# A decoder block on one core: the second convolution pair on the unnormalised input, GpSimd's powers in written order, and two pairs with one seven-product chunk

## The chip, the cores and the metric

The kernel runs on one core of one Trainium2 chip. The metric is device time in microseconds (us), from one launch of the whole program. Before the change the median of three runs is 2031.65 us (2030.2 to 2033.77). The engines are named as in the profile: PE is TensorE (PEld its weight loads), DVE is VectorE, ACT is ScalarE, POOL is GpSimd, SP the queue that issues most of the loads.

## The reference, cut to what matters

One layer of a decoder trunk on 256 tokens of width 2048 (float32):

```
h = rmsnorm(x, norm_mix)                       # x * rsqrt(mean(x^2) + eps) * gain
proj = h @ w_in                                # 2048 columns in, 15360 out
   -> differential attention (8 heads, two maps each, causal, rmsnorm per head)
   -> u = ca * sigmoid(cb); causal depthwise convolution of 31 taps over u; layernorm; silu
   -> retention in chunks of 128 (8 heads), normalised per head, times silu(rg)
   -> three sigmoid gates
x = x + (g0*(ya @ w_br0) + g1*(yb @ w_br1) + g2*(yr @ w_br2)) @ w_out
x = x + cross_attention(rmsnorm(x), rmsnorm(mem))      # 4 heads, 256 memory tokens, wq wkv wo
x = x + (silu(a) * b) @ w2,   a, b = rmsnorm(x) @ w13  # hidden 5632
out = rmsnorm(x, norm_final)
```

The row factor of an rmsnorm can be taken out of a product: (x * r * gain) @ W equals r times ((x * gain) @ W), so a product may be computed on x * gain and multiplied by r when it leaves the accumulator.

## The kernel before

**Products.** Every float32 operand is split into a high part (rounded to fp32r) and a low part (the rest), and a product is three matmuls: high by high, high by low, low by high. A weight matrix is cut into column blocks of 512, and each block into four chunks of 512 rows; a chunk is loaded in halves of 512 KB (tile `raw`, ten buffers, issued by SP through `ld`). ACT makes the high part (`wh`, a cast), DVE the low part (`wl`, a subtraction); both have five buffers. A unit is one such half or one factor of a chunk, with its matmuls; a half with both token tiles is 12 matmuls of 128x512, a factor of a seven-product chunk is 6. `emit_unit` (line 306) first builds the parts of the four units that follow and then writes the matmuls of its own.

**Pairs of column blocks.** `pair` (line 405) computes two column blocks at once. Each of its four chunks is of one of two kinds, by the letters of a mode string. An N chunk is eight half-products: four units of 12 matmuls. An S chunk (`quad_jobs`, line 332) is seven factors, p1 to p7, of 6 matmuls each, put together by sums; it needs two DVE sums on `raw` (in f2 and f3), and two more loads of 512 KB that add into a `raw` tile on their way, issued by POOL through `gd`: f2 issues one for p7, f6 one for p4. An S chunk also needs sums of the activations (`factors`). The factors p1, p5, p6 and p7 are gathered in one-bank accumulators (`tp`), the two blocks in two two-bank accumulators (`mm`, two buffers). The names are `MODES2 = "SSNN"`, `MODES1 = "SNNN"`, `MODES0 = "NNNN"`. `pair_n` (line 481) is for a pair on activations that are not normalised yet: no S chunk; its block 0 is complete after 12 of its 16 units, and is evacuated there, and `after(c)` tells when a chunk of activations has been read for the last time.

**Normalising between pairs.** `normalise` (line 640) takes chunks of x * gain, multiplies them by the row factor r, and makes new high and low parts; it starts at its chunk `at`. `spread` brings r into the layout of the chunks by a small matmul. `Rstd` waits for r; `rstd_of` (line 515) computes r on DVE (scale and eps) and then POOL (a power of -0.5).

**The stages.** The kernel starts with blocks 8 and 6 of w_in (`pair_n`, the gate and the value of the first half of the convolution's channels) on `xa`, then blocks 9 and 7 (the second half) on the normalised `xn`, as two plain blocks; then the blocks of retention and attention (plain), the gates and branches (pairs), the memory's keys and values (four `pair`s on `mm`, line 1182), w_out, cross attention, and the feed-forward part: 11 pairs of w_13 (line 1419 and before; the first is a `pair_n` on `x2T`) with w_2 between.

**Tasks.** Work beside the products (evacuations, transposes, the convolution, statistics) is written as generators. `pump` (line 142) moves each of them one `yield` after every unit; `drain` runs one to its end. So a `yield` more puts what follows one unit later in the program.

**What sets the order.** The program is planned before it runs: for each engine the planner orders the instructions by a model of time, and among ready ones takes the one written first. Two rules hold against that freedom. `keep_in_program_order` ties an instruction to the one written before it on its engine: `gd` and `ld` always use it, the power in `rstd_of` does not. And the buffers of one pool tag are handed out in the order in which the program first writes them: of the 392 tiles of tag s4 (28 buffers, the tile `s` of the profile) none is first written ahead of one that is written earlier in the program.

```
L519  nc.gpsimd.tensor_tensor(out=dst, in0=v, in1=nhalf[:, :w], op=ALU.pow)
L881  pair_n([w_in[8, c] ...], [w_in[6, c] ...], xa, ev_cb(0, rsx), ev_ca(0, rsx),
             normalise(xa, xn, Rstd(rsx, lambda: drain(st_task)), (), 1))
L883  win(9, 7, MODES0, ev_cb(1), ev_ca(1))
```

Of the kernel before, what the change touches and what calls it, by code (L numbers as in the profile page):

```python
# [13 lines left out]
ALU = mybir.AluOpType  # L14
AX = mybir.AxisListType

D = 2048
# [40 lines left out]
def trunk(ctx, tc, xT, xtok, memT, memtok, w_in, w_br, w_out, w_q, w_kv, w_o, w_13, w_2,  # L58
# [88 lines left out]
    def drain(g):  # L147
        if g in first:
            drain(first.pop(g))
        if g in active:  # L150
            settle(cap[0] - wants[g], g)
            while step(g):
                pass
# [327 lines left out]
    def pair_n(W0, W1, acts, evac0, evac1, after):  # L481

        ps0, ps1 = {}, {}
        u0, u1 = [], []
        for c in range(2):
            u0 += half_jobs(ps0, [W0[c]], [acts[c]])
            u1 += half_jobs(ps1, [W1[c]], [acts[c]])
            call(lambda c=c: after(c))
        u0 += half_jobs(ps0, W0[2:], acts[2:])
        call(lambda: evac0(ps0["m"]))  # L490
        for c in range(2, 4):
            u1 += half_jobs(ps1, [W1[c]], [acts[c]])
            call(lambda c=c: after(c))
        call(lambda: evac1(ps1["m"]))
        close(u0 + u1)
# [19 lines left out]
    def rstd_of(dst, src, scale, w):  # L515

        v = TN(w)
        ve.tensor_scalar(out=v, in0=src, scalar1=scale, scalar2=EPS, op0=ALU.mult, op1=ALU.add)
        nc.gpsimd.tensor_tensor(out=dst, in0=v, in1=nhalf[:, :w], op=ALU.pow)  # L519

    def actT_part(a, r, g, c, ks):
        if a.hi is None:
# [173 lines left out]
    def tok_stats(src, dst, eng):  # L696

        parts = cpool.tile([P, 4, 2], F32, name=nm("parts"))
        for n in range(4):
            r = S4([P, 2, 512])  # L700
            eng(out=r, in_=src[n])
            yield
            sumsq(r, parts[:, n, :])
            yield
        ss = TN(2)
        ve.tensor_reduce(out=ss, in_=parts.rearrange("p n t -> p t n"), op=ALU.add, axis=AX.X)
        rstd_of(dst, ss, 1.0 / D, 2)

    def start_task():
        for c in range(2, 4):  # L710
# [71 lines left out]
    def ev_cb(i, rs=None):  # L782
        def f(ps):
            if rs is not None:
                drain(st_task)
            cv["s", i] = act(ps, AF.Sigmoid, rs)
        return f
# [50 lines left out]
    def conv_norm():  # L838
        ys = [cv[("y", 0)], cv[("y", 1)]]
        bn = TN(24)  # L840
        for t in range(2):
            for i in range(2):
                o = (2 * t + i) * 6
                ve.bn_stats(out=bn[:, o:o + 6], in_=ys[i][:, t, :])
        mv = TN(4)
        for t in range(2):
            ve.bn_aggr(out=mv[:, 2 * t:2 * t + 2], in_=bn[:, 12 * t:12 * t + 12])
        rs = TN(2)
        rstd_of(rs, mv.rearrange("p (t s) -> p t s", t=2)[:, :, 1], 1.0, 2)
        yield  # L850
        for i in range(2):
            for t in range(2):
                ve.tensor_scalar(out=ys[i][:, t, :], in0=ys[i][:, t, :], scalar1=mv[:, 2 * t:2 * t + 1],
                                 scalar2=rs[:, t:t + 1], op0=ALU.subtract, op1=ALU.mult)
        yield
        for i in range(2):
            z = cv["z", i] = S4([P, 4, 256])
            src = blk(ys[i])
            for pr in range(2):
                tp = TP().rearrange("p (k c) -> p k c", k=2)  # L860
                for k in range(2):
                    for t in range(2):
                        pe.transpose(tp[:, k, t * P:(t + 1) * P], src(2 * pr + k, t), ident)
                yield 1
                for k in range(2):
                    c = 4 * i + 2 * pr + k
                    sc.activation(z[:, 2 * pr + k, :], tp[:, k, :], AF.Silu, scale=pc("lg", c), bias=pc("lb", c))
                tp = None
                yield
# [3 lines left out]
    def win(n0, n1, modes, evac0, evac1):  # L873
# [3 lines left out]
        else:  # L877
            block(w_in, n0, xn, evac0)
            block(w_in, n1, xn, evac1)

    pair_n([w_in[8, c] for c in range(4)], [w_in[6, c] for c in range(4)], xa, ev_cb(0, rsx), ev_ca(0, rsx),  # L881
           normalise(xa, xn, Rstd(rsx, lambda: drain(st_task)), (), 1))
    win(9, 7, MODES0, ev_cb(1), ev_ca(1))  # L883


    def ev_rope(store, key, half, ro):
# [47 lines left out]
    def ret_task(g, st):  # L934
        drain(st["qt"])
        drain(st["kt"])
        q, k, v, sg, dm = st["q"], st["k"], st["v"], st["g"], st["d"]
        o = S4([P, 2, 512])
        yield
        for h in range(4):  # L940
            s = TP()
            pe.matmul(s[:, 0:256], k[:, h, 0:P], q[:, h, :], start=True, stop=True)
            pe.matmul(s[:, 256:384], k[:, h, P:256], q[:, h, P:256], start=True, stop=True)
            yield 1
            p = SM(384)
            ve.tensor_tensor(out=p[:, 0:256], in0=s[:, 0:256], in1=dm[:, h, :], op=ALU.mult)
            ve.tensor_tensor(out=p[:, 256:384], in0=s[:, 256:384], in1=dm[:, h, 0:P], op=ALU.mult)
            s = None
            yield
            c = slice(h * P, (h + 1) * P)  # L950
            av = TP()
            pe.matmul(av[:, 0:P], p[:, 0:P], v[:, 0, c], start=True, stop=True)
            pe.matmul(av[:, P:256], p[:, P:256], v[:, 0, c], start=True, stop=False)
            pe.matmul(av[:, P:256], p[:, 256:384], v[:, 1, c], start=False, stop=True)
            yield 1
            sc.copy(o[:, :, c], av[:, 0:256].rearrange("p (t c) -> p t c", t=2))
            av = None
        q = k = v = dm = None
        st.clear()
        yield  # L960
        mv = TN(16)
        for t in range(2):
            for h in range(4):
                bn = TN(6)
                ve.bn_stats(out=bn, in_=o[:, t, h * P:(h + 1) * P])
                i = (4 * t + h) * 2
                ve.bn_aggr(out=mv[:, i:i + 2], in_=bn)
            yield
        rs = TN(8)
        rstd_of(rs, mv.rearrange("p (t s) -> p t s", s=2)[:, :, 1], 1.0, 8)  # L970
        yield
        for t in range(2):
            for h in range(4):
                i = 4 * t + h
                c = slice(h * P, (h + 1) * P)
                ve.tensor_scalar(out=o[:, t, c], in0=o[:, t, c], scalar1=mv[:, 2 * i:2 * i + 1],
                                 scalar2=rs[:, i:i + 1], op0=ALU.subtract, op1=ALU.mult)
            ve.tensor_tensor(out=o[:, t, :], in0=o[:, t, :], in1=sg[:, t, :], op=ALU.mult)
            yield
        sg = None  # L980
        yield from transposed(yr[g], blk(o), lambda kt: pc("gn", 4 * g + kt))
# [16 lines left out]
    def diff_task(g, st):  # L998
# [64 lines left out]
        ms = TN(8)  # L1063
        ve.tensor_reduce(out=ms, in_=sq.rearrange("p t (h c) -> p (t h) c", h=4), op=ALU.add, axis=AX.X)
        rs = TN(8)
        rstd_of(rs, ms, 1.0 / P, 8)
        yield
        for t in range(2):
            for h in range(4):
# [107 lines left out]
    for m, dst in ((0, kM), (4, vM)):  # L1177
        for h in (0, 2):
            if m == 4 and h == 2:
                call(mT_factors)  # L1180
            w0, w1 = ([w_kv[m + n, c] for c in range(4)] for n in (h, h + 1))
            pair(w0, w1, mm, MODES2, ev_kv(dst[h]), ev_kv(dst[h + 1]))
    call(lambda: [setattr(a, k, None) for a in mm for k in ("hi", "lo", "shi", "slo")])


    def residual(W, acts, xin, aT, gname, rs, parts, spill=None):

        xs = [None] * 4

        def ev(nb):  # L1190
            def f(ps):
                r = xin(nb)
                ve.tensor_tensor(out=r, in0=ps, in1=r, op=ALU.add)
                xs[nb] = r
                if spill is not None:
                    xs[nb] = None
                    gd(out=spill[nb], in_=r)

                def gen():
                    sumsq(r, parts[:, nb, :])  # L1200
                    yield from transposed(aT[nb], blk(r), lambda kt: pc(gname, 4 * nb + kt))
                aT[nb].task = spawn(gen())
                if nb == 3:
                    def gen2():
                        yield
                        yield
                        ss = TN(2)
                        ve.tensor_reduce(out=ss, in_=parts.rearrange("p n t -> p t n"), op=ALU.add, axis=AX.X)
                        rstd_of(rs, ss, 1.0 / D, 2)
                    rst[gname] = spawn(gen2())  # L1210
            return f
        return xs, ev
# [197 lines left out]
    def ffn_pairs(r):  # L1410
        for i in r:
            w0, w1 = ([w_13[n, c] for c in range(4)] for n in (i, 11 + i))
            if i == 0:
                pair_n(w0, w1, x2T, ev_a(i, rs2), ev_b(i, rs2), after2)
            else:
                pair(w0, w1, x2n, MODES2, ev_a(i), ev_b(i))

    def load_x2(nbs):
        for nb in nbs:
# [157 lines left out]
```

## Time and profile before

| | |
|---|---|
| three timed runs | 2031.65 us median (2030.2 to 2033.77) |
| the profiled execution's own time | 2031.24 us |
| its span, first to last instruction | 2029.5 us |
| mean granted TensorE clock | 0.991 |
| instructions with a record | PE 9069, DVE 2049, ACT 1344, POOL 176 |
| PE, DVE, ACT, POOL busy | 1990.1, 1680.8, 1122.2, 133.1 us |

All times inside the program are from the start of the span. A granted clock of 1.00 is the higher of TensorE's two levels (2.4 GHz), 0.50 the lower one (1.2 GHz). A line such as L86 is that of a helper through which most instructions pass, so rows are told apart by their tiles. The profile of one execution has records of nearly all instructions; a few matmuls can be missing.

### The profile page before, as it was taken

The page shows a single profiled execution, that of the slowest core. Times are in us where ns is not written, and L with a number is a line of the kernel's source. Part 1 is how long each engine was busy: PE and PEld are TensorE (multiplying, and loading weights), DVE is VectorE, ACT ScalarE, POOL GpSimd, SP SyncE. Part 2 cuts the span into 40 slices and gives each one's busy share as a digit, 9 for nine tenths or more (in the row PEclk, how much of TensorE's full clock was granted, in tenths as well). Part 3 has the DMA queues.
Part 4 walks back from the last instruction along what each step waited for, and adds up shares of the span by engine and source line. Part 5 has one row for each costly group of instructions (what it writes and reads, how often), then busy time and mean ns, then how long its engine had stood idle before and what let it go on. Part 6 is the DMA issues. An engine that isn't in the chain of part 4 may idle for free.

```text
span 2029.5 us, 25287 instructions
## 1 busy us (share of the span) xinstructions
PE 1990.1 (98%) x9069; PEld 1641.5 (81%) x9069; DVE 1680.8 (83%) x2049; ACT 1122.2 (55%) x1344; POOL 133.1 (7%) x176
## 2 busy tenths in 40 slices
PE   9999999999999999999999999998999999999998
PEld 7788888888788887778888888886888888878886
DVE  6996689777887787988988565898988899889974
ACT  6434343547465556555656554665655566555653
POOL 0000000000100001011010000100011101011000
PEclk9999999999999999999999999998999999999999
DMA  9555555554677788689999643967899888998891
GB/s 370 189 194 188 176 181 165 181 168 149 176 220 239 243 257 248 226 240 280 284 279 307 208 159 125 288 184 212 226 283 297 257 260 237 289 295 258 262 318 67
DMA packets 128861, 465.97 MB, mean 230 GB/s; under 512 B 14432, under 2 KB 14688, under 8 KB 128736
## 3 DMA queue, kind: packets, MB, share of 16 engines
q1 hardware_dynamic: 105552, 380.46, 53.2%
q0 software_dynamic: 23040, 83.90, 19.5%
q8 instruction: 71, 1.16, 0.2%
q14 instruction: 54, 0.44, 0.1%
q10 hardware_dynamic: 144, 0.01, 0.0%
HBM read 451.73 MB, written 12.58 MB: 229 GB/s over the span
## 4 chain that ended last, share of the span: by engine, by line
PE 50%; issue 9%; DVE 6%; DMA 5%; POOL 1%; ACT 1%; ACTq 0%; POOLq 0%; DVEq 0%
PE mm L86 38%; PE tp L86 12%; DMA raw<-in_w 4%; DVE wl L86 3%; DVE s L86 3%; DMA raw<-in_w_out 1%; DVE raw L86 1%; ACT wh L86 1%; POOL raw L94 1%; DMA s<-in_memtok 0%; DMA raw<-in_w_in 0%; ACT s L86 0%; ACTq L1572 0%; POOL s L94 0%; POOL x2d L94 0%
## 5 line engine op out<-in xcount | busy, mean ns | idle before, releaser
L86 PE MATMUL mm<-wh,s 128*128 128x512 f32 x4528 | 1440.1, 393 | 22.5 <-ACT wh L86 8.7
L86 ACT CAST wh<-raw 128x1024 fp32r<-128x1024 f32 (+1 forms) x861 | 893.6, 1051 | 754.3 <-PE mm L86 462.7
L86 DVE TENSOR_TENSOR wl<-raw,wh 128x1024 fp32r<-128x1024 f32 (+1 forms) x861 | 1030.1, 1220 | 265.2 <-ACT wh L86 252.0
L86 PEld LDWEIGHTS mm<-wh,s 128*128 128x128 f32 x4528 | 854.5, 189 | 204.8 <-ACT wh L86 13.5
L86 PE MATMUL mm<-wl,s 128*128 128x512 f32 x2264 | 889.5, 393 | 7.6 <-DVE wl L86 7.4
L86 PEld LDWEIGHTS mm<-wl,s 128*128 128x128 f32 x2264 | 428.0, 189 | 100.7 <-DVE wl L86 13.2
L86 PE MATMUL tp<-wh,s 128*128 128x512 f32 x896 | 298.5, 392 | 0.0
L86 PEld LDWEIGHTS tp<-wh,s 128*128 128x128 f32 x896 | 168.2, 188 | 34.7 <-issue 0.3
L86 PE MATMUL tp<-wl,s 128*128 128x512 f32 x448 | 174.5, 389 | 0.0
L86 DVE TENSOR_TENSOR s<-s,s 128x1024 f32<-128x1024 f32 (+4 forms) x144 | 141.4, 990 | 5.8 <-ACT s L86 4.0
L86 DVE TENSOR_TENSOR raw<-raw,raw 128x1024 f32<-128x1024 f32 x104 | 126.0, 1220 | 0.5
L86 DVE TENSOR_TENSOR s<-tp,s 128x512 f32<-128x512 f32 (+1 forms) x166 | 110.0, 685 | 19.0 <-PE tp L86 14.2
L86 DVE SCALAR_TENSOR_TENSOR s<-s,prm_t,s 128x256 fp32r<-128x256 f32 (+24 forms) x256 | 105.5, 469 | 0.0
L86 DVE TENSOR_TENSOR s<-mm,s 128x1024 f32<-128x1024 f32 (+1 forms) x71 | 84.4, 1190 | 21.7 <-PE mm L86 21.3
L86 PEld LDWEIGHTS tp<-wl,s 128*128 128x128 f32 x448 | 84.2, 188 | 16.8
L86 ACT ACTIVATE s<-s 128x512 f32<-128x512 f32 (+1 forms) x60 | 46.2, 771 | 64.3 <-DVE s L86 53.9
L94 POOL DMA_DIRECT2D raw<-in_w x56 | 49.4, 882 | 439.4 <-DVE wl L86 187.9
L86 PE MATMUL tp<-cst_t,s 128*128 128x128 f32 x408 | 57.2, 273 | 0.0
L86 PEld LDWEIGHTS tp<-cst_t,s 128*128 128x128 f32 x408 | 48.7, 141 | 9.2 <-issue 0.5
L86 PE MATMUL tp<-s,s 128*128 128x256 f32 (+4 forms) x348 | 54.1, 314 | 0.0
L86 PEld LDWEIGHTS tp<-s,s 128*128 128x128 f32 (+1 forms) x348 | 46.4, 189 | 5.9 <-issue 0.7
L86 ACT COPY s<-tp 128x512 f32<-128x512 f32 (+1 forms) x69 | 35.8, 529 | 21.5 <-PE tp L86 20.0
(88 smaller groups left out, 499.3 us busy)
## 6 DMA issues: line engine op xcount, KB each, us to landing
raw<-in_w SPq DMA_DIRECT2D x264, 512.0 KB, 6.7
raw<-in_w_in SPq DMA_DIRECT2D x239, 512.0 KB, 4.5
raw<-in_w_kv SPq DMA_DIRECT2D x64, 512.0 KB, 6.3
raw<-in_w POOLq DMA_DIRECT2D x56, 512.0 KB, 8.5
raw<-in_w_br SPq DMA_DIRECT2D x48, 512.0 KB, 5.9
raw<-in_w_out SPq DMA_DIRECT2D x32, 512.0 KB, 7.8
raw<-in_w_q SPq DMA_DIRECT2D x32, 512.0 KB, 4.9
raw<-in_w_o SPq DMA_DIRECT2D x32, 512.0 KB, 4.0
```

The source lines that it names most:

```text
L86: i = f(*a, **k)
L94: tc.keep_in_program_order(nc.gpsimd.dma_start(**kw))
```

## The change

In five edits:

```diff
 def rstd_of(dst, src, scale, w):
         v = TN(w)
         ve.tensor_scalar(out=v, in0=src, scalar1=scale, scalar2=EPS, op0=ALU.mult, op1=ALU.add)
-        nc.gpsimd.tensor_tensor(out=dst, in0=v, in1=nhalf[:, :w], op=ALU.pow)
+        yield
+        yield
+        tc.keep_in_program_order(nc.gpsimd.tensor_tensor(out=dst, in0=v, in1=nhalf[:, :w], op=ALU.pow))
...
-        rstd_of(dst, ss, 1.0 / D, 2)
+        yield from rstd_of(dst, ss, 1.0 / D, 2)
...
-    pair_n([w_in[8, c] for c in range(4)], [w_in[6, c] for c in range(4)], xa, ev_cb(0, rsx), ev_ca(0, rsx),
-           normalise(xa, xn, Rstd(rsx, lambda: drain(st_task)), (), 1))
-    win(9, 7, MODES0, ev_cb(1), ev_ca(1))
+    for n, after in ((0, lambda c: None),
+                     (1, normalise(xa, xn, Rstd(rsx, lambda: drain(st_task)), ()))):
+        pair_n([w_in[8 + n, c] for c in range(4)], [w_in[6 + n, c] for c in range(4)], xa,
+               ev_cb(n, rsx), ev_ca(n, rsx), after)
...
-            pair(w0, w1, mm, MODES2, ev_kv(dst[h]), ev_kv(dst[h + 1]))
+            pair(w0, w1, mm, MODES2 if m or h else MODES1, ev_kv(dst[h]), ev_kv(dst[h + 1]))
...
-                pair(w0, w1, x2n, MODES2, ev_a(i), ev_b(i))
+                pair(w0, w1, x2n, MODES1 if i == 1 else MODES2, ev_a(i), ev_b(i))
```

The other callers of `rstd_of` (the convolution's layernorm, retention, differential attention, the two residuals) are changed to `yield from` in the same way. The second pair is evacuated with the row factor, as the first: two ACT instructions instead of one, and two DVE instructions instead of one; the normalisation starts in the second pair, after its first chunk.

## Rows read from the trace of the kernel before

**Rows 1.** Page, part 1: busy time, share of the span, instructions.
```profile
PE 1990.1 (98%) x9069; PEld 1641.5 (81%) x9069; DVE 1680.8 (83%) x2049; ACT 1122.2 (55%) x1344; POOL 133.1 (7%) x176
```

**Rows 2.** Waits of PE, whole span: us in total, times, longest.
```profile
PE mm L86 <- ACT wh L86: 8.7, 9, 3.6
PE mm L86 <- DVE wl L86: 7.4, 12, 1.5
PE mm L86 <- DVE s L86: 7.0, 1, 7.0
PE mm L86 <- ACT s L86: 6.7, 2, 4.7
```

**Rows 3.** Stretches of 40 us: busy (instructions) by engine, granted clock, DMA.
```profile
40.00:80.00 40.00, 35.34 (x151) 28.74 (x150) 34.36 (x42) 21.04 (x23) 0.70 (x1) 0.91 0.64 233
...
520.00:560.00 40.00, 35.27 (x152) 28.23 (x152) 30.31 (x46) 21.00 (x31) 3.37 (x3) 0.93 0.66 193
560.00:600.00 40.00, 40.00 (x175) 33.04 (x175) 33.80 (x32) 24.14 (x26) 1.69 (x2) 0.98 0.73 220
...
680.00:720.00 40.00, 40.00 (x178) 33.14 (x177) 31.59 (x29) 21.40 (x22) 1.70 (x2) 1.00 0.73 224
...
840.00:880.00 40.00, 34.32 (x139) 26.49 (x138) 36.64 (x41) 19.91 (x22) 3.43 (x4) 0.87 0.67 166
...
1400.00:1440.00 40.00, 32.98 (x137) 26.77 (x136) 34.93 (x39) 19.75 (x22) 3.42 (x4) 0.87 0.69 188
```

**Rows 4.** Instructions in order of time, all engines, 40 to 90 us.
```profile
53.84 1.04 ACT L86 CAST s<-s 128x1024 fp32r<-128x1024 f32 x1
...
56.19 1.26 ACT L86 ACTIVATE s<-mm,rsx 128x512 f32<-128x512 f32 x2
...
57.51 0.79 PE L86 MATMUL mm<-wh,s 128*128 128x512 f32 x1 [4.66 <-ACT s L86]
```

**Rows 5.** POOL's instructions in order of time: start, us, idle before.
```profile
33.41 0.70 POOL L519 TENSOR_TENSOR rsx<-tn,nhalf 128x2 f32<-128x2 f32 x1 [32.56 <-DVE tn L86]
...
528.88 0.86 POOL L94 DMA_DIRECT2D raw<-in_w_in  x1 [14.54 <-DVE wl L86]
545.35 1.66 POOL L519 TENSOR_TENSOR tn<-tn,nhalf 128x8 f32<-128x8 f32 x1 [15.61 <-DVE tn L86]
546.97 0.89 POOL L94 DMA_DIRECT2D raw<-in_w_in  x1
...
804.80 1.62 POOL L519 TENSOR_TENSOR rsm<-tn,nhalf 128x2 f32<-128x2 f32 x1 [8.02 <-DVE tn L86]
...
1319.27 0.71 POOL L519 TENSOR_TENSOR rs<-tn,nhalf 128x2 f32<-128x2 f32 x1 [1.43 <-DVE tn L86]
```

**Rows 6.** Chain of waits, 500 to 570 us: start, us, what.
```profile
546.97 7.08 DMA raw<-in_w_in
```

**Rows 7.** ACT in order of time, around 1353 us.
```profile
1353.60 1.27 ACT L86 ACTIVATE s<-mm,rs 128x512 f32<-128x512 f32 x2
```

**Rows 8.** Waits of PE, 840 to 880 us.
```profile
PE mm L86 <- DVE wl L86: 3.1, 3, 1.5
PE mm L86 <- ACT s L86: 2.1, 1, 2.1
PE mm L86 <- ACT wh L86: 0.5, 1, 0.5
```

**Rows 9.** DVE in order of time, four stretches.
```profile
536.49 2.36 DVE L86 TENSOR_TENSOR wl<-raw,wh 128x1024 fp32r<-128x1024 f32 x2 [1.98 <-ACT wh L86]
...
804.62 2.35 DVE L86 TENSOR_TENSOR wl<-raw,wh 128x1024 fp32r<-128x1024 f32 x2
...
863.01 3.48 DVE L86 TENSOR_TENSOR wl<-raw,wh 128x1024 fp32r<-128x1024 f32 x3
...
1410.51 2.35 DVE L86 TENSOR_TENSOR s<-mm,s 128x1024 f32<-128x1024 f32 x2
```

**Rows 10.** Chain of waits, 1300 to 1425 us.
```profile
1328.43 21.79 PE mm L86 x96
...
1379.25 9.38 DMA raw<-in_w
```

More of the change, by code (lines that the diff above doesn't have):

```diff
@@ L848, in conv_norm @@
         rs = TN(2)
-        rstd_of(rs, mv.rearrange("p (t s) -> p t s", t=2)[:, :, 1], 1.0, 2)
+        yield from rstd_of(rs, mv.rearrange("p (t s) -> p t s", t=2)[:, :, 1], 1.0, 2)
         yield
@@ L969, in ret_task @@
         rs = TN(8)
-        rstd_of(rs, mv.rearrange("p (t s) -> p t s", s=2)[:, :, 1], 1.0, 8)
+        yield from rstd_of(rs, mv.rearrange("p (t s) -> p t s", s=2)[:, :, 1], 1.0, 8)
         yield
@@ L1065, in diff_task @@
         rs = TN(8)
-        rstd_of(rs, ms, 1.0 / P, 8)
+        yield from rstd_of(rs, ms, 1.0 / P, 8)
         yield
@@ L1208, in gen2 @@
                         ve.tensor_reduce(out=ss, in_=parts.rearrange("p n t -> p t n"), op=ALU.add, axis=AX.X)
-                        rstd_of(rs, ss, 1.0 / D, 2)
+                        yield from rstd_of(rs, ss, 1.0 / D, 2)
                     rst[gname] = spawn(gen2())
```

## The prediction

> **What bounds the kernel now.** I read the page first, then PE's waits, then stretches of 40 us, then single engines in order of time where a stretch stood out. PE is busy for 98% of the span [rows 1], and where nothing disturbs it a run of 96 matmuls takes 21.79 us, 0.227 us each [rows 10]; so 6 matmuls cost 1.36 us and 12 cost 2.72. The kernel is PE's, and can gain only where PE waits or runs at the lower clock. PE's named waits are 29.8 us in all [rows 2], and the stretches show where: PE falls below 40 us in 40 to 80, 520 to 560, 840 to 880 and 1400 to 1440, and in each the granted clock falls too, to 0.91, 0.93, 0.87 and 0.87, while an undisturbed stretch has 178 instructions at 1.00 [rows 3]. A lower mean clock is time at half speed: 0.09 x 40 / 0.5 = 7.2 us of 40 to 80; half of that part of it in which PE worked is lost. Read together, four places cost:
>
> A, the end of the first pair: 4.7 us of waiting [rows 4] and 2.4 us of clock (4.9 of the 7.2 us worked).
> B, a pair of gates: 3.6 us waiting for a cast, the longest of its row [rows 2]; clock 5.6 us at half in 520 to 560 and 1.6 in the stretch behind it [rows 3], 6.0 worked, 3.0 lost.
> C, the first pair on the memory: 3.1 + 2.1 + 0.5 = 5.7 us waiting [rows 8]; clock 10.4 us at half, 8.0 worked, 4.0 lost.
> D, the second pair of the feed-forward part: 7.0 us at one place [rows 2], 1.8 us shortly before it (part of the 8.7 for casts in the same group), clock 10.4 us at half, 5.8 worked, 2.9 lost.
>
> Together 22.8 us of waiting and 12.3 us of clock, 35.1 us. The change touches each of the four.
>
> **A, the second pair on the unnormalised input.** PE stands at 52.85 for an accumulator that ACT's sigmoid must empty. The row factor had been there since 34.1 [rows 5], and block 0 was complete four units (10.9 us) before. The sigmoid comes directly behind the cast that makes xn's second chunk [rows 4]: that cast is written earlier in the program, the tiles of its tag are handed out in that order, and it waits for DVE. In the change the first pair has no normalisation in it, so the tiles ahead of the sigmoid are those of the statistics alone. Those come some three weight loads later than before, as nothing drains them after the second chunk any more; at about 1.3 us per issue on SP and the later pow this puts the row factor near 40 us, where block 0 ends at 42 and PE wants the buffer at 52.9. What is queued behind the sigmoid on ACT are casts four units ahead of PE. So I take the 7.1 us as gone. Normalising moves into the second pair: the same four chunks, no instruction more. The nearest row is the pair in the feed-forward part with this very form, normalising from its first chunk on: there the evacuation runs at 1353.60, as its block ends, and PE does not wait at the pair's end [rows 7]. The evacuations cost ACT 1.26 instead of about 1.05 us and DVE 0.2 more; both lie beside matmuls. Bounds: nothing gained, if the wait appears at the end of the second pair, to 7.1 us.
>
> **B, the power in order.** POOL issues an accumulating load at 528.88, then holds a power whose input comes at 545.3, and issues the next accumulating load right behind it at 546.97 [rows 5]. That load takes 7.08 us [rows 6] and is what the casts for p4 wait for, at 554.1. Its own input was there long before: the low part of p6 is in the two subtractions that end at 538.85 [rows 9], so it could have gone 8.1 us earlier and landed at 546, while PE stops only at 551.7. In the program the power is written after one unit and the load during the next; two yields put the power behind it, and tied in order it can't float ahead again. What waits for the power now: its own head normalisation, 60 units away from its use. The 3.6 + 3.0 = 6.6 us go. Bounds: nothing to 6.6. The other eight powers: none stands ahead of a load that PE waits for; the one of the memory's statistics has the four memT loads behind it, which start when it ends, at 806.4 [rows 5]. If two units' delay were real there, 5.4 us of work would slip into C; nothing else is written on POOL between its old place and its new one, so I take zero.
>
> The Trainium skill's page "DMA: Bandwidth & Descriptors", "Anatomy of one DMA", prices a GpSimd-issued load at 2.0 us plus its bytes at 436 GB/s: an estimate of 3.2 us for 512 KB, by which the load issued at 546.97 lands at 550.2, before PE needs it, and B's cause lies elsewhere. The trace has 7.08 us for this load, so it decides for the load; the page's way is part of the third rival.
>
> A power beside DVE is the point where a rule speaks against the edit. The power of two columns takes 0.71 us at 1319 but 1.62 at 804.80, just behind the start of a subtraction at 804.62 [rows 5, 9]. The Trainium skill's page "SBUF — State Buffer", "Who interferes with whom", says that a GpSimd instruction that reads SBUF and a DVE instruction with two SBUF inputs shut each other out for a whole instruction, whoever is first; the trace agrees for POOL. Were DVE the one shut out, a power of eight columns (1.66 us) would hold up one subtraction, and B would give 1.7 us back: 2004.2 us instead of my sum.
>
> **C and D, one seven-product chunk.** An S chunk replaced by an N chunk costs PE 8 x 6 matmuls instead of 7 x 6, 1.36 us a pair, 2.7 in both, always on the path. It takes from the pair three casts on ACT, three subtractions and two sums on DVE, at 1.14 us each back to back (3.48 us for three, the last with its full length) [rows 9], 5.7 us, and two accumulating loads. Activation sums are still made for the later pairs.
>
> In C, DVE is busy 36.6 of 40 us [rows 3]. Up to p6, PE works 10 x 1.36 + 4 x 2.72 = 24.5 us and waits 5.7, so DVE needed 30.2 us; the pair's own 14 subtractions and 4 sums are 20.5 of that, the rest 9.7. With one S chunk these are 11 and 2, 14.8 us; with the 9.7 that makes 24.5 us beside PE's 5 x 1.36 + 6 x 2.72 = 23.1. So 1.4 us of waiting stay, in pieces too small to bring the clock down. The last wait of C, for the high part of the sums of chunk 1 (2.1 us), goes wholly, since this pair doesn't use them. C gives 9.7 - 1.4 = 8.3.
>
> In D, PE first waits for a cast behind an accumulating load (9.38 us) [rows 10]. DVE starves with it, catches up without a pause, and gets to the first block's sum only at 1410.51 [rows 9]; PE starts at 1411.87 when that frees the accumulator. With one S chunk two loads of four remain, p4's comes three 12-matmul units earlier with respect to its use, and the pair ends in six units of 2.72 us with 1.14 us of DVE each. I leave half of the first wait (0.9) and take the rest, 10.8, as gone. If the pair behind it then starts short of DVE, some returns: bounds for C and D together nothing to 21.4, before the 2.7.
>
> **The sum.** 35.1 - 1.4 - 0.9 - 2.7 = 30.1; the planner orders everything behind the first edit anew, and against small waits of the kind already there (1.0, 0.7, 0.6 us at single places) I put 1.0. 29.1 us off the profiled execution's own 2031.24 give 2002.1; the median of the runs is 0.4 above it, so 2002.5 us.
>
> **Rivals.** First, DVE stays the bound in C and D: with 83% over the span [rows 1] and 92% in C, the time is taken by the pair behind. Half of the 21.4 us stays, 8.4 more than I left: 2011. For it: both waits end on DVE. Against: in 680 to 720, a stretch of pairs, DVE has 31.6 of 40 us and PE no wait [rows 3]. Second, the sigmoid's wait moves to the end of the second pair, where the same tiles are written ahead of it: 2009.6. Against: xn's second chunk is there written two units before the sigmoid and has no late row factor to wait for. Third, the load in B still stands behind the power, or its length isn't the cause, and that edit doesn't do what it says: 2009.1. Fourth, slower: in the second pair DVE has the convolution's first half as well, 124 operations of 0.42 us, 52 us, spawned before the normalisation. Placed ahead of it, with 16 subtractions (18 us), they end near 58 + 70 = 128 us, and xn's first chunk, needed at 96.5, comes at about 132: 35 us of waiting and 3 of clock, which with B, C and D as forecast is 2047. It makes the kernel slower once that chunk is later than about 116 us (19 us of waiting and 3 of clock against 22.0 from the rest). Against: two such operations are written per unit, and they have not held PE up at 80 to 160 us, where they fill DVE.
>
> **Chances.** Forecast 0.56 (1998 to 2008), first rival 0.16, second 0.08, third 0.08, fourth 0.05, several at once (2014 to 2028) 0.07. A measurement of this kernel can't tell less than 0.2% (4.1 us) from no change. Faster by more: the first four and half of the last, 0.91; same 0.03; slower 0.06. The range takes the first three rivals and part of the mixtures: 1996 to 2020.
>
> **What would show it.** A: the sigmoid at 42 to 46 us, no PE wait near 53 and none near 97. B: the pow behind the fourth load of its pair, that load within 1 us of p6's low part, the clock at 1.00 from 520 to 600. C and D: four POOL loads fewer (POOL 172), DVE and ACT down by ten less one and six less one, 12 matmuls more, and the clock at 1.00 in 840 to 880 and 1370 to 1440. The prediction is wrong if PE's waits still add up to over 15 us, or the clock still falls at one of the four places.

## The result, and the profile after

Four timed runs of the changed kernel have a median of 2001.7 us (1998.88 to 2005.18), four of the kernel before 2030.93 us: a ratio of 0.9857 (95% interval 0.9835 to 0.9879), 29.0 us (24.6 to 33.5) faster. The forecast was 2002.5 us. The profiled execution, the fastest of the four, took 1998.88 us, its span is 1997.1 us, 32.4 less than that of before, and its granted clock 0.999.

The page's first part; it answers to [rows 1]:

```profile
PE 1979.9 (99%) x9081; PEld 1636.8 (82%) x9081; DVE 1666.9 (83%) x2040; ACT 1120.4 (56%) x1343; POOL 129.8 (6%) x172
```

The waits of PE over the whole span, in total, times, longest; all of them [rows 2]:

```profile
PE mm L86 <- DVE wl L86: 4.4, 7, 1.0
PE mm L86 <- ACT wh L86: 3.3, 5, 1.2
PE tp L86 <- DVE parts L86: 1.2, 1, 1.2
```

All waits together were 31.0 us before: 29.8 in the four rows of [rows 2], and 1.2 in a fifth row, which is the last row here and has not changed. Now they are 8.9 us, the longest 1.2. The two rows for an `s` tile, 7.0 and 6.7 us, are gone altogether.

The stretches of 40 us at the four places, columns as in [rows 3]. The program runs ahead of before by what it has gained, about 7 us behind A, 15 behind B and 23 behind C:

```profile
40.00:80.00 40.00, 40.00 (x184) 33.19 (x183) 31.51 (x52) 20.70 (x23) 0.00 (x0) 1.00 0.72 250
...
520.00:560.00 40.00, 38.80 (x179) 31.85 (x178) 34.86 (x44) 25.87 (x29) 3.38 (x3) 1.00 0.83 253
560.00:600.00 40.00, 40.00 (x179) 33.10 (x178) 33.26 (x30) 20.42 (x20) 3.46 (x4) 1.00 0.77 202
...
840.00:880.00 40.00, 39.03 (x176) 31.82 (x175) 36.80 (x39) 23.79 (x27) 3.68 (x5) 1.00 0.80 249
...
1360.00:1400.00 40.00, 40.00 (x182) 33.20 (x181) 39.21 (x41) 24.08 (x26) 3.44 (x4) 1.00 0.80 228
1400.00:1440.00 40.00, 40.00 (x182) 33.17 (x181) 38.81 (x39) 25.22 (x27) 3.45 (x4) 1.00 0.86 260
```

PE does 176 to 184 instructions in each, where the four lowest of before had 137 to 152, and the clock is 1.00 throughout. DVE is as full as before in these stretches (39.2 of 40 us at D), though over the whole program it has 13.9 us less to do [rows 1]; but PE no longer stands behind it.

ACT in order of time around the first pair's evacuation [rows 4]:

```profile
41.53 1.28 ACT L86 ACT_TABLE_LOAD   x1 [1.71 <-PE mm L86]
42.83 1.26 ACT L86 ACTIVATE s<-mm,rsx 128x512 f32<-128x512 f32 x2
```

POOL in order of time [rows 5]:

```profile
38.88 0.70 POOL L521 TENSOR_TENSOR rsx<-tn,nhalf 128x2 f32<-128x2 f32 x1 [38.03 <-DVE tn L86]
...
522.14 0.86 POOL L94 DMA_DIRECT2D raw<-in_w_in  x1 [17.54 <-DVE wl L86]
525.74 0.86 POOL L94 DMA_DIRECT2D raw<-in_w_in  x1 [2.73 <-DVE wl L86]
531.87 1.66 POOL L521 TENSOR_TENSOR tn<-tn,nhalf 128x8 f32<-128x8 f32 x1 [5.28 <-DVE tn L86]
```

The chain of waits, 500 to 570 us [rows 6]:

```profile
524.22 1.24 DVE wl L86
...
525.74 10.27 DMA raw<-in_w_in
...
537.21 3.06 PE mm L86 x12
```

The sigmoid starts at 42.83 us, as soon as ACT has its table, and not at 56.19. The load for p4 goes out 3.6 us after the one ahead of it, where 18.1 us lay between the two before, and the power follows it. It takes 10.27 us on its way, and 1.2 us of PE's wait, which ends at 537.21, are left of 3.6.

### The profile page after: what moved, and what is told of

It is laid out like the page before. It is cut to its first block, busy times and chain, and to the rows that moved or that the text cites. A ratio compares the mean times of both kernels' runs of the same rounds, so it can differ in the third digit from the quotient of the medians.

```text
span 1997.1 us, 25285 instructions
## 1 busy us (share of the span) xinstructions
PE 1979.9 (99%) x9081; PEld 1636.8 (82%) x9081; DVE 1666.9 (83%) x2040; ACT 1120.4 (56%) x1343; POOL 129.8 (6%) x172
## 4 chain that ended last, share of the span: by engine, by line
PE 79%; issue 9%; DVE 6%; DMA 4%; POOL 1%; ACT 1%; SPq 0%; ACTq 0%; POOLq 0%; DVEq 0%
PE mm L86 64%; PE tp L86 15%; DVE wl L86 3%; DVE s L86 2%; DMA raw<-in_w 2%; DMA raw<-in_w_kv 1%; DMA raw<-in_w_in 1%; POOL raw L94 1%; DVE raw L86 1%; ACT wh L86 1%; DMA s<-in_memtok 0%; SPq L97 0%; POOL s L94 0%; ACTq L1575 0%; POOL x2d L94 0%
## 5 line engine op out<-in xcount | busy, mean ns | idle before, releaser
L86 PE MATMUL tp<-wh,s 128*128 128x512 f32 x864 | 288.5, 392 | 0.0
L86 PEld LDWEIGHTS tp<-wh,s 128*128 128x128 f32 x864 | 162.2, 188 | 33.1
L86 PE MATMUL tp<-wl,s 128*128 128x512 f32 x432 | 168.1, 389 | 0.0
L86 DVE TENSOR_TENSOR raw<-raw,raw 128x1024 f32<-128x1024 f32 x100 | 121.0, 1216 | 0.4
L86 DVE SCALAR_TENSOR_TENSOR s<-s,prm_t,s 128x256 fp32r<-128x256 f32 (+25 forms) x256 | 105.8, 461 | 0.0
```

Of the source, the lines that this page charges most:

```text
L86: i = f(*a, **k)
```

## The experiments

A ratio is always to the kernel before, run in turn on the same chip; below 1 is faster.

**Each edit alone.** Four kernels, each the kernel before with one part of the change.

```diff
-    pair_n([w_in[8, c] for c in range(4)], [w_in[6, c] for c in range(4)], xa, ev_cb(0, rsx), ev_ca(0, rsx),
-           normalise(xa, xn, Rstd(rsx, lambda: drain(st_task)), (), 1))
-    win(9, 7, MODES0, ev_cb(1), ev_ca(1))
+    for n, after in ((0, lambda c: None),
+                     (1, normalise(xa, xn, Rstd(rsx, lambda: drain(st_task)), ()))):
+        pair_n([w_in[8 + n, c] for c in range(4)], [w_in[6 + n, c] for c in range(4)], xa,
+               ev_cb(n, rsx), ev_ca(n, rsx), after)
```

> The kernel before with the first edit alone: the second convolution pair on the unnormalised input. Theory (the sigmoid stood behind the cast of xn's second chunk; each place of loss has its own cause): the wait near 53 us and the clock loss of 40 to 80 us go, 7.1 us, and the other three places (520 to 560, 840 to 880, 1400 to 1440) keep theirs: 2030.9 - 7.1 = 2023.8 us, ratio 0.9965. Rival 1 (the wait only moves to the end of the second pair, near 97 us): no gain, ratio 1.000. Rival 2 (the gain of the whole change comes from the new order that the planner makes behind the first edit, not from the places): the other three places get better here too, ratio below 0.994.

Measured: 0.9962 (0.9949 to 0.9976), 7.7 us. PE has no wait between 40 and 130 us. The other places keep theirs: 3.4 us for p4's cast, 5.2 us in 830 to 960, 7.0 us for the sum in D. The theory holds, both rivals fall.

```diff
-        nc.gpsimd.tensor_tensor(out=dst, in0=v, in1=nhalf[:, :w], op=ALU.pow)
+        yield
+        yield
+        tc.keep_in_program_order(nc.gpsimd.tensor_tensor(out=dst, in0=v, in1=nhalf[:, :w], op=ALU.pow))
```

> The kernel before with the powers alone: two yields ahead of each power, and the power in written order. Theory (the power at 545 us holds up the accumulating load behind it): that load is issued some 8 us earlier, the 3.6 us wait shrinks to 1.5 or less and the clock is 1.00 from 520 to 600 us; 5.0 to 6.6 us, ratio 0.9968 to 0.9975. Rival 1 (the load is late for another reason, or its own length is the cause): the wait stays, ratio 0.9995 to 1.0005. Rival 2 (the delayed powers hold up the memory's statistics, and the loads of memT behind them): 5 us more of waiting between 840 and 880 us, ratio 1.000 although the first wait goes.

Measured: 0.9964 (0.9953 to 0.9976), 7.3 us. The wait is 1.1 us, the clock 1.00 from 520 to 600 us, and the waits of 830 to 960 us are 5.8 us in all, against 5.7 before: the later powers hold up nothing.

```diff
-            pair(w0, w1, mm, MODES2, ev_kv(dst[h]), ev_kv(dst[h + 1]))
+            pair(w0, w1, mm, MODES2 if m or h else MODES1, ev_kv(dst[h]), ev_kv(dst[h + 1]))
```

> The kernel before with one seven-product chunk instead of two in the first pair on the memory, alone. Theory (that pair is short of DVE time): 8.3 us of waiting and clock go, 1.4 us of products come, ratio 0.9966 (6.9 us); the waits of 840 to 880 fall from 5.7 to about 1.4 us. Rival 1 (DVE's lack is only taken by the next pair): the waits of 880 to 960 us grow by as much, ratio 1.0000 to 1.0007. Rival 2 (the cause is the late start of the memory's activations, not the pair's own DVE work): the waits on the activations' parts stay, at least 2.1 us of them, and the gain is at most 3 us, ratio 0.9985.

Measured: 0.9975 (0.9965 to 0.9985), 5.1 us; the forecast 0.9966 lies in the interval. The waits of 840 to 880 us are 2.5 us (1.5 and 1.0), not 1.4, and the clock there is 1.00. The 1.5 us is for a cast behind an accumulating load of 8.54 us. The next pair pays nothing: its stretch has 178 instructions at 1.00 and no wait.

```diff
-                pair(w0, w1, x2n, MODES2, ev_a(i), ev_b(i))
+                pair(w0, w1, x2n, MODES1 if i == 1 else MODES2, ev_a(i), ev_b(i))
```

> The kernel before with one seven-product chunk instead of two in the second pair of the feed-forward part, alone. Theory: the 7.0 us wait for the first block's sum and half of the 1.8 us ahead of it go, with the clock's 2.9 us, less 1.4 us of products: 9.4 us, ratio 0.9954. Rival 1 (DVE stays the bound there): half of it, ratio 0.998. Rival 2 (the third pair takes the lack): new waits of 5 us or more in 1440 to 1480 us, ratio 0.9985 or above. If the four parts are independent, the four gains add up to the whole change's 29.2 us, within 4 us; if they hang on one another, they add up to 20 us or less.

Measured: 0.9947 (0.9935 to 0.9958), 10.8 us. No wait at all between 1280 and 1450 us. The four gains add up to 30.9 us, the whole change gives 29.0: the four parts add up within the intervals.

**Was it the tile?** The kernel before, with the sigmoid's tile taken at the program's start.

```diff
         spawn(st_task)
+        cv["early"] = S4([P, 2, 512])
+        nc.gpsimd.memset(cv["early"][:, 0, 0:1], 0.0)
...
-        s = S4([P, 2, 512])
+        s = cv.pop("early")
```

> The kernel before, with one thing changed: the tile that the first pair's sigmoid writes is taken, and touched by a one-column memset on GpSimd, at the start of the program, so that its turn among the s4 tiles comes first. The pairs stay as they were; the sum is the reference's. Theory (the sigmoid stood at 56 us only because its tile is handed out behind that of xn's second chunk): the sigmoid runs at 42 to 46 us, right behind block 0, the 4.7 us wait and its 2.4 us of clock go: 2030.4 - 7.1 = 2023.3 us, ratio 0.9965, as much as the second-pair edit alone gave (0.9962). Rival 1 (ACT's queue or the row factor holds the sigmoid, the tile does not): sigmoid and wait stay, ratio 1.000. Rival 2 (the sigmoid comes early, but the normalised chunks then come late for the next block): a new wait of 3 us or more between 57 and 100 us, ratio 0.998 or above.

Measured: 0.9973 (0.9962 to 0.9984), 5.5 us. ACT in order of time:

```profile
42.77 1.27 ACT L86 ACTIVATE s<-mm,rsx 128x512 f32<-128x512 f32 x2
...
54.68 1.05 ACT L86 CAST s<-s 128x1024 fp32r<-128x1024 f32 x1 [0.62 <-DVE s L86]
```

Nothing else of the evacuation was touched, and the sigmoid moves from 56.19 to 42.77 us, ahead of the cast (now at 54.68) that it stood behind. PE's wait of 4.7 us shrinks to 0.3. So it was the tile's turn, as the prediction read it from two neighbouring rows.

**The power: yields or order?**

```diff
+        yield
+        yield
         nc.gpsimd.tensor_tensor(out=dst, in0=v, in1=nhalf[:, :w], op=ALU.pow)
```

> The kernel before with the two yields ahead of each power, but the powers not tied to the written order. Theory (what counts is that the power is written behind the accumulating load): the load is written earlier, the planner issues it first, and the 3.6 us wait shrinks to 1.2 as with both halves of the edit; ratio 0.9964. Rival (the tie is what keeps the power from floating ahead of the load again): the power stands in front of the load, the wait stays at 3.6 us, ratio 1.000.

```diff
-        nc.gpsimd.tensor_tensor(out=dst, in0=v, in1=nhalf[:, :w], op=ALU.pow)
+        tc.keep_in_program_order(nc.gpsimd.tensor_tensor(out=dst, in0=v, in1=nhalf[:, :w], op=ALU.pow))
```

> The kernel before with the powers tied to the written order, without the yields. Theory: the power is still written ahead of the load of p4, so it still stands in front of it; wait 3.6 us, clock 0.93 to 0.96 in 520 to 560 us, ratio 1.000 (0.999 to 1.001). Rival 1 (the tie alone is the cure): ratio 0.9964. Rival 2 (a power tied in front of loads that could pass it before holds up more loads): slower, ratio 1.001 to 1.004, with the new wait behind a power in 450 to 600 us.

Measured: the yields alone 0.9960 (0.9947 to 0.9972), the tie alone 1.0008 (1.0000 to 1.0017). POOL with the yields alone:

```profile
532.70 0.85 POOL L94 DMA_DIRECT2D raw<-in_w_in  x1 [2.77 <-DVE wl L86]
538.84 2.57 POOL L521 TENSOR_TENSOR tn<-tn,nhalf 128x8 f32<-128x8 f32 x1 [5.29 <-DVE tn L86]
```

and with the tie alone:

```profile
545.30 1.67 POOL L519 TENSOR_TENSOR tn<-tn,nhalf 128x8 f32<-128x8 f32 x1 [15.60 <-DVE tn L86]
546.93 0.89 POOL L94 DMA_DIRECT2D raw<-in_w_in  x1
```

The yields carry the edit: with them the power is written behind the load and runs behind it. The tie does nothing here, neither as a cure nor as a harm. But the yields move more than the power. With them the subtraction that the load waits for ends at 532.6 us and not at 538.85, and PE comes to its wait for the cast at 543.0 and not at 551.7. How much of the gain is the power's place in POOL's queue, and how much this new order on DVE and PE, was not tried apart.

**DVE's work or the loads?** First, in the changed kernel, DVE's work comes back at C and D without the loads: five subtractions of plain halves are done twice in each of the two pairs.

```diff
             lo_of(u, rv)
+            if u.get("twice"):
+                lo_of(u, rv)
...
+        if twice:
+            for u in [u for u in us if all(k == "n" and len(u["prods"]) == 2 for *_, k in u["prods"])][:5]:
+                u["twice"] = True
```

> The changed kernel with DVE's work put back, but not the loads: in the first pair on the memory and in the second of the feed-forward part, five of the plain halves' subtractions are done twice (the same result), 5 x 1.24 = 6.2 us of DVE in each pair, about what the second seven-product chunk took there; no accumulating load and no cast comes back. Theory (in both places PE waited because DVE had more work in the pair than the pair lasts): the waits return, 4 to 6 us in each pair and 2 to 3 us of clock with each, 12 to 18 us: 2013.5 to 2019.5 us, ratio 0.9917 to 0.9946. Rival (they came from the late accumulating loads, behind which DVE starved): at most 3 us come back, ratio 0.9857 to 0.9872. Mixed: the one place returns and the other does not, ratio 0.988 to 0.991.

Measured: 0.9907 (0.9894 to 0.9919), 0.0050 or 10 us more than the changed kernel, less than the theory's range and more than the rival's; the mixed case. Waits of PE in C, 800 to 880 us:

```profile
PE mm L86 <- DVE wl L86: 2.4, 2, 1.5
PE tp L86 <- DVE s L86: 1.8, 1, 1.8
PE mm L86 <- DVE s L86: 1.8, 1, 1.8
```

and in D, 1330 to 1420 us:

```profile
PE mm L86 <- DVE wl L86: 2.4, 2, 1.5
```

In C the work alone brings 6.0 us of waiting, as much as the 5.7 of before, though partly at other instructions (two waits for a sum, and none for the activations' parts): there DVE's amount of work is enough to make the loss. In D the same amount costs only 2.4 us, with the clock at 1.00, against 8.8 and a lower clock. So there the loads had to be tried.

The next two kernels belong together: the changed kernel without its last edit, and the same without the two accumulating loads of that pair's second seven-product chunk. The second kernel leaves out two addends of that chunk, so that pair's result lacks them.

```diff
-                pair(w0, w1, x2n, MODES1 if i == 1 else MODES2, ev_a(i), ev_b(i))
+                pair(w0, w1, x2n, MODES2, ev_a(i), ev_b(i))
```

> The changed kernel without its last edit: two seven-product chunks again in the second pair of the feed-forward part. It is the control of the next kernel. Theory (the four parts are independent): the 7 us wait and its clock come back, 1.4 us of products go; by the edit done alone (ratio 0.9947, 10.8 us) this is 2001.7 + 10.8 = 2012.5 us, ratio 0.991. Rival (the other edits have eased this place too): the wait is under 4 us, ratio 0.988 or below.

```diff
-            gd(out=t["b"], in_=b22, accum_op=ALU.add)
+            if acc:
+                gd(out=t["b"], in_=b22, accum_op=ALU.add)
...
-            gd(out=t["a"], in_=b21, accum_op=ALU.add)
+            if acc:
+                gd(out=t["a"], in_=b21, accum_op=ALU.add)
...
-                pair(w0, w1, x2n, MODES1 if i == 1 else MODES2, ev_a(i), ev_b(i))
+                pair(w0, w1, x2n, MODES2, ev_a(i), ev_b(i), i != 1)
```

> As the control, but the second seven-product chunk of that one pair is computed without its two accumulating loads (two addends of that chunk are missing in the pair's output): DVE, ACT and PE have all the work of two seven-product chunks, POOL two loads less. Theory (in this place DVE starved behind the accumulating load of 9.38 us, and the work alone is not too much): no wait of 2 us or more in 1370 to 1430 us, 2001.7 - 1.4 = 2000.3 us, ratio 0.985 (up to 0.987). Rival (DVE's work is too much for the pair, with or without the loads): the wait for the first block's sum stays, 5 to 7 us with 2 to 3 us of clock, 2007 to 2010 us, ratio 0.9885 to 0.990.

Measured: 0.9895 (0.9880 to 0.9910) and 0.9893 (0.9878 to 0.9909): the loads make no difference in time that these intervals can tell. The first lies between its theory, 0.991, and its rival, 0.988: beside the other three edits the last one is worth 0.0038, some 8 us, where alone it gave 10.8, and the 7.0 us wait comes back in full. The second has the time of its rival and not of its theory. PE's waits, 1330 to 1420 us, with the loads:

```profile
PE mm L86 <- DVE s L86: 7.0, 1, 7.0
PE mm L86 <- ACT wh L86: 1.8, 1, 1.8
```

and without the two:

```profile
PE mm L86 <- DVE s L86: 6.2, 1, 6.2
```

The wait for the cast goes with the loads, as it must. The long one stays. My theory for D, that DVE starved behind the load of 9.38 us and so came late to the sum, has fallen: without that pause PE's wait for the sum is only 0.8 us shorter. DVE in order of time, without the loads, shows what it does instead:

```profile
1376.35 2.35 DVE L86 TENSOR_TENSOR raw<-raw,raw 128x1024 f32<-128x1024 f32 x2
1378.61 1.22 DVE L86 TENSOR_TENSOR wl<-raw,wh 128x1024 fp32r<-128x1024 f32 x1
1379.75 1.28 DVE L86 TENSOR_TENSOR s<-tp,s 128x512 f32<-128x512 f32 x2
1380.95 2.35 DVE L86 TENSOR_TENSOR wl<-raw,wh 128x1024 fp32r<-128x1024 f32 x2
...
1384.41 2.35 DVE L86 TENSOR_TENSOR wl<-raw,wh 128x1024 fp32r<-128x1024 f32 x2
1386.68 1.22 DVE L86 TENSOR_TENSOR raw<-raw,raw 128x1024 f32<-128x1024 f32 x1
1387.82 2.35 DVE L86 TENSOR_TENSOR s<-mm,s 128x1024 f32<-128x1024 f32 x2
```

The last row holds both blocks' sums, back to back. Ahead of them stand three sums on `raw` tiles that belong to the next pair (POOL issues that pair's first two accumulating loads right behind the first two, at 1378.10 and 1379.23). PE stands from 1383.0. With one such chunk and the doubled subtractions, nearly as much work, the planner had laid the sums otherwise (DVE, in the kernel with the work put back):

```profile
1380.12 1.23 DVE L86 TENSOR_TENSOR s<-mm,s 128x1024 f32<-128x1024 f32 x1
1381.25 3.50 DVE L86 TENSOR_TENSOR wl<-raw,wh 128x1024 fp32r<-128x1024 f32 x3
1384.65 2.37 DVE L86 TENSOR_TENSOR raw<-raw,raw 128x1024 f32<-128x1024 f32 x2
```

There the first block's sum comes ahead of the next pair's. So it does in the changed kernel:

```profile
1366.61 1.21 DVE L86 TENSOR_TENSOR s<-mm,s 128x1024 f32<-128x1024 f32 x1
...
1373.41 2.35 DVE L86 TENSOR_TENSOR raw<-raw,raw 128x1024 f32<-128x1024 f32 x2
...
1378.23 1.22 DVE L86 TENSOR_TENSOR s<-mm,s 128x1024 f32<-128x1024 f32 x1 [0.20 <-PE mm L86]
```

So D is not the amount alone and not these loads, and what the rows show in their place is where the first block's sum stands in DVE's queue. That this order makes the wait is read from the rows and not shown: two seven-product chunks with the sum laid ahead were not tried.

**More of the same?** If PE is short only of time, another seven-product chunk where DVE has room should give more. First a third one in the last five pairs of gates:

```diff
-    for c in SC:
+    for c in range(3):
         call(later(xn[c]))
...
-            win(18 + 4 * br + nb, ..., MODES2 if bi or nb else MODES0, ev_gate(nb), ev_gate(nb + 1))
+            win(18 + 4 * br + nb, ..., "SSSN" if bi or nb else MODES0, ev_gate(nb), ev_gate(nb + 1))
```

> The changed kernel with a third seven-product chunk in the last five pairs of gates (and the sums of xn's third chunk, which it needs). Theory (there DVE has 31.6 of 40 us and PE does not wait, so 5.7 us more of DVE a pair fit in): 5 x 1.36 = 6.8 us of products go, small waits of 1 to 2 us come: 1996 us, ratio 0.983. Rival (more accumulating loads, later loads and DVE's work in bursts bring waits and clock losses back): 3 us or more per pair in 560 to 880 us, no gain or slower than the changed kernel, ratio 0.986 to 0.993.

Then one in the first pair of gates:

```diff
+    call(later(xn[0]))
     win(4, 5, MODES0, ev_dv(0), ev_dv(1))
+    call(later(xn[1]))
...
-    for c in SC:
-        call(later(xn[c]))
...
-            win(18 + 4 * br + nb, ..., MODES2 if bi or nb else MODES0, ev_gate(nb), ev_gate(nb + 1))
+            win(18 + 4 * br + nb, ..., MODES2 if bi or nb else MODES1, ev_gate(nb), ev_gate(nb + 1))
```

> The changed kernel with one seven-product chunk in the first pair of gates, which had none, and the sums of xn's first two chunks made before and after the block that precedes it. Theory: one product less (1.4 us) and DVE's sums moved to a stretch with room: 2000.3 us, ratio 0.985. Rival (between 480 and 560 us DVE and ACT have the attention's tasks, whose end is needed soon after): a wait of 2 us or more there, no gain, ratio 0.986 to 0.988.

Measured: 0.9984 (0.9973 to 0.9996) and 0.9913 (0.9898 to 0.9927), both slower than the changed kernel's 0.9857. Both are slower than even their rivals' ranges. In the first PE's waits rise to 35.7 us in all, against 6.8 us of products saved. Both meet B again. POOL with three chunks:

```profile
550.02 2.57 POOL L521 TENSOR_TENSOR tn<-tn,nhalf 128x8 f32<-128x8 f32 x1 [11.92 <-DVE tn L86]
552.55 0.89 POOL L94 DMA_DIRECT2D raw<-in_w_in  x1
```

With one chunk in the first pair it is the same (the power at 542.71, the load at 545.24): the loads that PE wants next are written behind the power again, and two yields are no longer enough. How much of the loss this makes was not tried by itself.

## Why the prediction was right, step by step

**The sum.** 29.1 us were forecast, 29.0 came. Part by part, with what each edit gave alone: A 7.1 forecast, 7.7 (4.9 to 10.4) measured; B 6.6, and 7.3 (4.9 to 9.5); C 8.3 less 1.4 of products, and 5.1 (3.0 to 7.1); D 10.8 less 1.4, and 10.8 (8.5 to 13.2). So no term is off by more than its interval; C lies at the edge of it. That the sum meets the measured gain within 0.1 us is luck: the terms are off by 0.6 to 1.8 us, C too high and the others too low, and the interval of the gain reaches some 4.5 us to either side. PE's waits of before were 31.0 us in all, not 29.8: the fifth row was left out, but it lies in none of the four places.

**A** was right in its mechanism, which the early tile shows by itself. The row factor is ready at 39.6 us ("near 40"), and the sigmoid runs at 42.83 ("42 to 46"). The second pair's runs at 89.75, and PE does not wait at that pair's end: the second rival did not come. Nor the fourth: xn's first chunk is ready by 92.9, and no wait follows.

**B** was right that the power stood in front of the load and that the wait goes with it, and 1.2 us of the 3.6 stay: I let the freed load take the 7.08 us of before, and it took 10.27, with another accumulating load issued 3.6 us ahead of it. The third rival did not come: the load goes out ahead of the power. An estimate of 3.2 us for such a load, worked out from the Trainium skill's page "DMA: Bandwidth & Descriptors", "Anatomy of one DMA", is farther from the 10.27 us than the 7.08 was. What the prediction did not see is the new order around the power: it let the load go at 538.85 and PE stop at 551.7, and with the 6.7 us gained in A added (528.88 less 522.14), the load went at 532.5 and PE stopped at 542.7. Nor did I see that the yields alone carry the edit; I left both halves together.

**C** was right, in size too: 1.4 us of waiting were to stay, 1.0 is there in the changed kernel and 2.5 with the edit alone. Of these 2.5, 1.5 are for a cast behind an accumulating load, which the term, made of DVE's work alone, does not have.

**D** was right in size and wrong in its cause. I left 0.9 us of the first wait; none remains. The step "DVE starves with it, catches up without a pause, and gets to the first block's sum only at 1410.51" reads the load as what made the sum late; with the load away 6.2 of the 7.0 us stay. In the changed kernel the first block's sum stands ahead of the next pair's sums (1366.61), and the second runs at 1378.23, as soon as PE has its block done. Whether the edit works by this order stays open.

**The first rival**, DVE as the bound with half of the gain lost, did not come, although DVE is as busy as before. **The planner's new order** had been given 1.0 us; outside B and C the waits are 6.7 us, against 8.2 outside the four places before (31.0 less 22.8), so it cost nothing here, though it was an order, not an amount, that made A and B and, by its rows, D. **The counts**: PE 12 more, POOL 4 fewer and DVE 9 fewer, as forecast; ACT one fewer, not five. Four more table loads of 1.28 us (17 instead of 13), which I had not counted, come in; ACT has room for them.

## What to carry to other kernels

When PE stands for an engine that is not full, look at what stands directly in front of the instruction it wants: here it was a tile's turn, a power in front of a load and, as the rows have it, two sums behind the next pair's preparations; the amount of work was enough by itself at one of the four places. Where a planner fixes each engine's order, take a part away and look at the order again before calling the work too much.

## What the runs showed of the hardware

**The same wait cost the clock twice as much in one execution as in another.** The wait at A is 4.7 us in the kernel before and in the one with the yields alone. Their stretches of 40 to 80 us have the same busy time of PE, but the granted clock of 0.91 [rows 3] means 7.2 us at the lower level, and this one, with the yields alone, 3.2 us:

```profile
40.00:80.00 40.00, 35.34 (x156) 28.87 (x155) 34.90 (x42) 21.31 (x24) 0.70 (x1) 0.96 0.64 240
```

Each is one profiled execution, so whether the kernel or the execution makes the difference is not shown. In one stretch idle time in pieces did not bring the clock down: with three seven-product chunks PE loses 4.6 us in 800 to 840, 2.8 us of it at one place, and keeps its clock:

```profile
800.00:840.00 40.00, 35.37 (x152) 27.63 (x151) 32.11 (x36) 25.14 (x37) 6.01 (x9) 1.00 0.98 338
```

**A power that began beside a subtraction took longer; a subtraction that began beside a power did not.** The power of eight columns took 1.66 us where DVE was idle as it began, and 2.57 with the yields alone (538.84, above), where a subtraction had begun 0.18 us before:

```profile
538.66 1.22 DVE L86 TENSOR_TENSOR wl<-raw,wh 128x1024 fp32r<-128x1024 f32 x1
```

The Trainium skill's page "SBUF — State Buffer", "Who interferes with whom", lets whichever is first hold up the other. In the changed kernel the power is first, 531.87 to 533.53, and this subtraction starts inside it and takes no longer than elsewhere:

```profile
532.81 1.23 DVE L86 TENSOR_TENSOR wl<-raw,wh 128x1024 fp32r<-128x1024 f32 x1 [1.02 <-ACT wh L86]
```

So only the half of the rule in which GpSimd is held up shows here, at one place each and as far as POOL's spans can be trusted, and the 1.7 us that the other half would have cost did not come.
